# A fixed step for every piece of the blocks' preparation, its products in TensorE's written order, and GpSimd's row operations moved from blocks 2 and 3 to block 1

## The chip, the core and the metric

The kernel runs on one core of a Trainium2 chip. A core has TensorE (PE, matrix products), VectorE (DVE), ScalarE (ACT), GpSimd (POOL) and SyncE (SP, which issues most loads). Each engine takes its own instructions one after the other, in the order of its queue, and waits on semaphores for the others. The metric is the device time of one execution in microseconds. The kernel before took 1632.62 us (median of 3 runs, 1624.2 to 1632.76).

## The reference

Two neural blocks in sequence on 512 positions of 1024 channels, all in 32-bit floats. The change lies in the first one's recurrent mixer, which runs over 256 context positions and then over the 512 positions, forwards and backwards, for 8 heads of 64 channels:

```
def step(S, inp):
    r_t, w_t, kk_t, b_t, v_t, k_t = inp
    sa = jnp.einsum("bhvk,bhk->bhv", S, kk_t)
    S = (S * w_t[:, :, None, :] - sa[..., None] * b_t[:, :, None, :]
         + v_t[..., None] * k_t[:, :, None, :])
    return S, jnp.einsum("bhvk,bhk->bhv", S, r_t)
...
cb, cc, cx, r, k, v, w_lo, a_lo, g_lo = split_proj(h @ lp["w_in"])
y, finals = rwkv_scans(r, k, v, w_lo, a_lo, lp, init)
y_conv = cb * shortconv1d(cc * cx, lp["conv_a_w"])
y_rwkv = rwkv_output(y, r, k, v, g_lo, lp)
return jnp.concatenate([y_conv, y_rwkv], axis=-1) @ lp["w_out"], finals
```

After it come an output projection, a convolutional feed-forward network, the second block (a gated linear recurrence, windowed attention and another feed-forward network) and a norm.

## The kernel before

`proj` (L301) projects the inputs with `w_in` in column tiles of 128. Each 32-bit operand is split into a high part (ScalarE, L183) and a rest (L184, usually VectorE), and a tile is 24 products (`mm3`). In the tiles below 12 and in tile 25 the rest of a tile's second half is made by GpSimd. The last part of `proj` is the short convolution: for j = 0 to 3 the tiles 4+j, 8+j and j. Beside the tiles runs `ada12`, 32 row loads of 512 KB each with one VectorE operation of 128x1024.

The recurrence is cut into chunks of 64 positions, 12 in each direction, and the heads into 4 blocks of 2 heads. `rwkv` (L489) runs one `stage` (L767) of 12 steps for each block j. A step takes one chunk of each direction: products on TensorE, four to six copies on ScalarE (`R` L804, `U` L810, the state `S` L821, the output `Y`), which each wait for the product before and are waited for by the next. `look` (L723) works ahead: for each pair of chunks it makes products into PSUM (`psc`), which VectorE masks into `AS` (L747, COPY_PREDICATED), and transposed keys (`pkt`), which ScalarE copies; `psc` and `pkt` share three banks, tag "sc". A stage's products and `look`'s bear the token "pe" and keep their written order on TensorE.

Before its stage each block needs `prep` (L560), a generator that stops 29 times, so that it runs in 30 pieces: pieces 1 to 16 load keys, decays and low-rank weights, make products `pb`, `pl` and `pa` (L582, L592, L644) in one PSUM bank, and fill `KB` and `KR`; pieces 17 to 30 are `inverse` (L666), which inverts the 24 triangular 64x64 matrices of `AK`. Its core are 62 row operations (L688, L689), each needing the one before, on VectorE for blocks 0 and 1 and on GpSimd for blocks 2 and 3 (L682). Two transposes (`F`, L691 and L692) on VectorE follow, then copies into `XT` and products `pt` and `po` (L708, L715), whose result completes `XT`, the operand of the stage's third group of products.

`prep(0)` runs as one run inside `proj`. Blocks 1 to 3 stand in one chain: `RC` = 5 pieces after each j of the convolution, then `RB` = 4, 2 pieces in each step of stages 0 and 1. What is left after stage 1 is written at once; from stage 2 on the chain holds `splits` (five splits for the output projection) and `first` (its first weight tile). In the written order a step has a priority, `base + 200*g`, and a piece one that is put 105 to 118 later (`PF`). The scheduler that orders each engine's instructions goes by these priorities and by its own idea of when an operand is ready; only instructions of one token keep their order among themselves. `gn` (L841) is the group norm of a finished block, spread over the next stage's steps; two of its operations, `ys` and the power `grs`, are GpSimd's.

Of the kernel before, what the change touches and what calls it, by code (L numbers as in the profile page):

```python
# [18 lines left out]
P = 128  # L19
# [103 lines left out]
class K:  # L123
# [177 lines left out]
    def proj(self):  # L301
        nc, A, r1, p0 = self.nc, self.A, self.r1, self.p0
# [6 lines left out]
        for k in range(KD):  # L309
            e = nc.scalar if k % 2 else nc.sync  # L310
# [26 lines left out]
        bcc, _ = self.rsqrt_bc(acc[:, 0:NC_], NC_, 1.0 / 1024, 1e-6, self.pp)  # L337
# [6 lines left out]
        hc = [t[:, i, :] for tag, n in (("KB10", 6), ("KB11", 6), ("KR10", 5)) for t in [self.pp.tile([P, n, NC_], F32R, tag=tag, name="hc", bufs=1)] for i in range(n)]  # L344
        hhi = [[None] * KD, hc[:KD]]
        hlo = [[None] * KD, hc[KD:2 * KD]]
        piece = lambda u, k0: self.wsplit(A["win"][u][:, k0:k0 + 4], 4, P, eng=nc.gpsimd if k0 and not 12 <= u < 25 else None)
        ahead = {(24, k0): piece(24, k0) for k0 in (0, 4)}
        G = self.pp.tile([P, KD, 2], F32, tag="bo", name="G", bufs=2)
        for kc in range(KD):  # L350
# [4 lines left out]
            for i in range(2):  # L355
                g, sh = G[:, kc, i:i + 1], self.mod[:, kc, i:i + 1]
# [11 lines left out]
        def rows(n):  # L368
            for _ in range(n):
                next(ada, None)  # L370

        def tile_of(u, x=True, c=True):
            rows(1 if 12 <= u < 25 else 2)
            ws = [ahead.pop((u, k0), None) or piece(u, k0) for k0 in (0, 4)]
            w = lambda k: ws[k // 4](k % 4)
            out = []
            for on, i, n in ((x, 0, NX), (c, 1, NC_)):
                if on:
                    pm = self.psmm(n)
# [76 lines left out]
                r, hs = slice(64 * (i % 2), 64 * (i % 2) + 64), slice(64 * (i // 2), 64 * (i // 2) + 64)  # L456
                nc.sync.dma_start(out=self.vD[hs, :, 2 * tb + i % 2, :], in_=t.rearrange("p (j c) -> p j c", c=P)[r, :, hs])
        self.sets1()
        self.todo = self.prep(1)
        px, = tile_of(25, c=False)  # L460
        nc.scalar.activation(out=self.sg, in_=px, func=AF.Tanh, scale=0.5)
        nc.vector.tensor_scalar(out=self.sg, in0=self.sg, scalar1=0.5, scalar2=0.5, op0=ALU.mult, op1=ALU.add)
        for j in range(4):
            t = self.zx[j]
            pcc, = tile_of(4 + j, c=False)
            nc.scalar.activation(out=t, in_=pcc, func=AF.Copy)
            pcx, = tile_of(8 + j, c=False)
            u = r1.tile([P, NX + 2], F32, tag="u", name="u", bufs=1)
# [6 lines left out]
            pcb, = tile_of(j, c=False)  # L475
            nc.vector.tensor_tensor(out=t, in0=t, in1=pcb, op=ALU.mult)
            for _ in range(self.RC):
                next(self.todo, None)
        for _ in ada:
            pass  # L480

# [7 lines left out]
    def rwkv(self, es, ep):  # L489
        nc, r2 = self.nc, self.r2  # L490
        st = lambda name, shape: r2.tile([P] + shape, F32, name=name)
        self.AS = [[st(f"AS{d}{i}", [2, 192]) for i in range(3)] for d in range(2)]
        self.RU = [[st(f"RU{d}{i}", [2, 64]) for i in range(2)] for d in range(2)]
        self.S0 = [[st(f"S0{d}{i}", [64]) for i in range(2)] for d in range(2)]
        self.C1, self.C2 = [[self.ps2.tile([P, 512], F32, name=f"c{i}{d}") for d in range(2)] for i in (1, 2)]
        for t in (*self.AS[0], *self.AS[1]):
            nc.vector.memset(t, 0.0)
        todo, gn = self.todo, iter(())
        self.cells, self.vt, self.ahd = {}, {}, self.look()
        self.load_v(0)  # L500
        for _ in range(8):
            next(self.ahd)
        self.outs = []
        for j in range(4):
            if j < 2:
                todo = chain(todo, self.prep(j + 2))
            gn = self.stage(j, todo, self.RB[j], gn)
# [12 lines left out]
        for _ in todo:  # L520
            pass

        for _ in range(3):
            next(gn)
        for pm, w in self.ahead:
            self.mm3(pm, [(*w(k), self.ahi[k], self.alo[k]) for k in range(7)], last=False)
        for _ in gn:
            pass

    def splits(self):  # L530
        for k in range(5):
            self.split(self.ahi[k], self.alo[k], self.zx[k])
            yield

# [25 lines left out]
    def prep(self, j):  # L560
# [26 lines left out]
        for d in range(2):  # L587
# [51 lines left out]
            for q in range(2):  # L639
                pa = psm(384, "pa")  # L640
                for c in range(6 * q, 6 * q + 6):
                    kp = krc[:, c, :] if c < 4 else krx[:, c - 4, 0, :]
                    lt, rt_ = (kp, kb[:, c, bs, :]) if d else (kb[:, c, bs, :], kp)
                    self.mmh(pa[:, (c - 6 * q) * 64:(c - 6 * q) * 64 + 64], lt, rt_)  # L644
                n = 12 * d + 6 * q
                self.copy(nc.scalar, self.AK[:, n:n + 6, :], pa.rearrange("p (c t) -> p c t", t=64))
                yield
        yield from self.inverse(j)

# [16 lines left out]
    def inverse(self, j):  # L666
# [5 lines left out]
        XT, AK = self.S[j]["XT"], self.AK  # L672
# [19 lines left out]
        nc.vector.transpose(out=F2.rearrange("p n j -> p j n"), in_=X.rearrange("p i j -> p j i"))  # L692
        yield
        D = slice(0, 12), slice(12, 24)
        for r, F in zip(D, (F1, F2)):
# [7 lines left out]
        for r in D:  # L703
            yield
            pt = ps("pt")
            for n in range(r.start, r.stop):
                for h in range(2):
                    nc.tensor.matmul(pt[b1[h], n - r.start, :], AK[b0[h], n, 32:64], F2[b0[h], n, :], start=True, stop=True)  # L708
            for h in range(2):
                self.copy(nc.scalar, T[b1[h], r, :], pt[b1[h]])  # L710
        yield
        po = ps("po")
        for c in range(12):
            for h in range(2):
                nc.tensor.matmul(po[b0[h], c, :], T[b1[h], c, :], F1[b1[h], c, :], start=True, stop=True)  # L715
                nc.tensor.matmul(po[b1[h], c, :], F1[b1[h], 12 + c, :], T[b1[h], 12 + c, :], start=True, stop=True)
# [6 lines left out]
    def look(self):  # L723
# [3 lines left out]
        for j in range(4):  # L727
            for i in range(6):
# [9 lines left out]
                for d, (c0, kb, krs, A) in enumerate(part):  # L738
                    ps = self.ps2.tile([P, 2, N], F32, tag="sc", name="psc", bufs=3)
                    for c in range(2):  # L740
                        if c:
                            yield
                        self.mmh(ps[:, c, 0:W], kb[:, c0 + c, d], krs[c], order="pe")
                        if x:
                            self.mmh(ps[:, c, W:N], kb[:, c0 + c, 1 - d], krs[c][:, 64:P], order="pe")
                    m = self.c(f"m{d}").bitcast(I32)[:, 0:N]
                    nc.vector.copy_predicated(A[:, :, 0:N], m.unsqueeze(1).to_broadcast([P, 2, N]), ps)  # L747
# [16 lines left out]
        self.nc.sync.dma_start(out=vt, in_=self.vD[:, j])  # L764
        self.vt[j] = vt

    def stage(self, j, todo, rb, gn):  # L767

        nc, r2 = self.nc, self.r2
        XT, PC = self.S[j]["XT"], self.S[j]["PC"]  # L770
# [15 lines left out]
        for g in range(12):  # L786
# [45 lines left out]
                    self.load_v(j + 1)  # L832
            with self.prio(at + self.PG):
                next(gn, None)
            for i in range(rb):
                with self.prio(at + self.PF[j] + i * self.PK // rb):
                    next(todo, None)
        self.tc.cur_priority = base + 12 * self.PK
        return self.gn(j, Y, self.S[j]["bo"], self.vt[j])

    def gn(self, j, Y, bo, vt):  # L841
# [50 lines left out]
        if j < 3:  # L892
            pg = gate()
        nc.vector.tensor_tensor(out=z, in0=pg, in1=z, op=ALU.mult)
        if j:
            self.split(self.ahi[4 + j], self.alo[4 + j], z)


# [562 lines left out]
```

## Time and profile before

The profiled execution took 1635.69 us (its span from the first to the last instruction 1633.9 us), 3.07 us over the median of the runs.

| stretch of the span (us) | what runs | length |
|---|---|---|
| 0 to 281.9 | `proj` with `prep(0)` and most of `prep(1)` | 281.9 |
| 281.9 to 351.5 | stage 0 | 69.6 |
| 351.5 to 443.9 | stage 1 | 92.4 |
| 443.9 to 524.7 | stage 2 | 80.8 |
| 524.7 to 565 | stage 3 | 40.3 |
| 565 to 1633.9 | the rest of both blocks | 1068.9 |

A stage begins here with its first copy `R` (L804). The profile counts an engine as busy while an instruction runs, not while it waits. TensorE's granted clock is given as a share of 2.4 GHz and takes two levels, 1.2 and 2.4 GHz, so a mean of 0.75 over a stretch is half its time at either level.

### The profile page before, as it was taken

Reading aid. Unit: us, or ns where it says so; the run is one execution under the profiler, and the core shown is the slowest. Engines: PE = TensorE matmul, PEld = TensorE weight load, DVE = VectorE, ACT = ScalarE, POOL = GpSimd, SP = SyncE. Lnnn points to the kernel's source line nnn. Section 1 sums busy time; section 2 is a strip of 40 time slices with the busy share of each in tenths; the row PEclk is TensorE's granted clock in tenths of the full one; section 3 lists DMA queues with packets and bytes.
Section 4 is the critical chain, followed back from the end, with each engine's and each line's share of the span. In section 5 each row is a group of like instructions: output and inputs, shape, how many; then the busy total and the mean of one; then the engine's idle time right before and its main releaser. Section 6 shows DMA issues by size and latency. Waiting matters only on the chain. (4 is left out here: it accounts for less than half of the span.)

```text
span 1633.9 us, 29054 instructions
## 1 busy us (share of the span) xinstructions
PE 1493.1 (91%) x12062; PEld 1236.5 (76%) x12062; DVE 960.7 (59%) x1554; ACT 631.5 (39%) x1258; POOL 211.6 (13%) x278
## 2 busy tenths in 40 slices
PE   4999699874849999999999998899999999999998
PEld 2877577864748899888888886787777888888886
DVE  3768956652423267888884437678975555554221
ACT  3524243452516443333333324334554333332122
POOL 1121122046280000000000003121200000000000
PEclk9999899776868999999999999999999999999999
DMA  9577522010002042232332332221022322323221
GB/s 340 184 260 223 147 92 86 4 44 2 4 11 95 18 130 78 92 103 91 103 90 91 98 98 79 78 65 52 27 60 86 100 90 91 103 91 101 93 84 58
DMA packets 62181, 152.84 MB, mean 94 GB/s; under 512 B 12641, under 2 KB 14433, under 8 KB 62049
## 3 DMA queue, kind: packets, MB, share of 16 engines
q1 hardware_dynamic: 58016, 143.95, 27.7%
q10 hardware_dynamic: 4032, 7.04, 1.3%
q8 instruction: 94, 1.54, 0.4%
q14 instruction: 39, 0.31, 0.1%
HBM read 143.10 MB, written 7.86 MB: 92 GB/s over the span
## 5 line engine op out<-in xcount | busy, mean ns | idle before, releaser
L183 ACT ACTIVATE whi<-w 128x1024 fp32r<-128x1024 f32 (+2 forms) x220 | 208.8, 950 | 448.6 <-PE pm L170 323.3
L184 DVE TENSOR_TENSOR wlo<-w,whi 128x1024 fp32r<-128x1024 f32 (+2 forms) x199 | 220.5, 1109 | 168.5 <-ACT whi L183 166.7
L169 PE MATMUL pm<-ahi,whi 128*128 128x512 f32 (+1 forms) x624 | 237.0, 380 | 3.0 <-DVE sh L1144 2.6
L170 PE MATMUL pm<-alo,whi 128*128 128x512 f32 (+1 forms) x624 | 235.5, 377 | 0.0
L171 PE MATMUL pm<-ahi,wlo 128*128 128x512 f32 (+1 forms) x624 | 234.7, 376 | 0.0
L170 PE MATMUL pm<-al,whi 128*128 128x512 f32 x352 | 140.3, 399 | 0.0
L169 PE MATMUL pm<-ah,whi 128*128 128x512 f32 x352 | 139.9, 397 | 0.0
L171 PE MATMUL pm<-ah,wlo 128*128 128x512 f32 x352 | 139.8, 397 | 0.0
L169 PEld LDWEIGHTS pm<-ahi,whi 128*128 128x128 f32 x624 | 118.0, 189 | 24.4 <-ACT sh L1159 3.0
L171 PEld LDWEIGHTS pm<-ahi,wlo 128*128 128x128 f32 x624 | 118.0, 189 | 21.1 <-issue 0.7
L170 PEld LDWEIGHTS pm<-alo,whi 128*128 128x128 f32 x624 | 117.9, 189 | 20.1 <-issue 0.7
L1017 DVE SCALAR_TENSOR_TENSOR cv<-pm,vec,cv 128x441 f32<-128x441 f32 (+2 forms) x176 | 121.0, 693 | 4.1
L169 PEld LDWEIGHTS pm<-ah,whi 128*128 128x128 f32 x352 | 66.5, 189 | 15.8
L171 PEld LDWEIGHTS pm<-ah,wlo 128*128 128x128 f32 x352 | 66.5, 189 | 15.7 <-issue 0.2
L170 PEld LDWEIGHTS pm<-al,whi 128*128 128x128 f32 x352 | 66.5, 189 | 15.7 <-issue 0.2
L169 PE MATMUL pm<-hhi,whi 128*128 128x512 f32 x176 | 73.3, 417 | 4.7 <-ACT whi L183 4.6
L171 PE MATMUL pm<-hhi,wlo 128*128 128x512 f32 x176 | 71.5, 406 | 1.4 <-DVE wlo L184 1.4
L170 PE MATMUL pm<-hlo,whi 128*128 128x512 f32 x176 | 71.2, 405 | 0.0
L169 PE MATMUL pd<-whi,gh 128*128 128x512 f32 x176 | 69.6, 396 | 0.0
L170 PE MATMUL pd<-wlo,gh 128*128 128x512 f32 x176 | 69.5, 395 | 0.0
L171 PE MATMUL pd<-whi,gl 128*128 128x512 f32 x176 | 69.5, 395 | 0.0
L169 PE MATMUL pm<-hh,whi 128*128 128x512 f32 x176 | 69.3, 394 | 0.0
(399 smaller groups left out, 3060.7 us busy)
## 6 DMA issues: line engine op xcount, KB each, us to landing
w<-in_fup SPq DMA_DIRECT2D x44, 512.0 KB, 3.7
adaw<-in_adat SPq DMA_DIRECT2D x32, 512.0 KB, 4.6
w<-in_win SPq DMA_DIRECT2D x44, 256.0 KB, 3.6
w<-in_wg SPq DMA_DIRECT2D x22, 512.0 KB, 3.7
w<-in_wu SPq DMA_DIRECT2D x22, 512.0 KB, 3.7
w<-in_wd SPq DMA_DIRECT2D x22, 512.0 KB, 3.7
w<-in_win SPq DMA_DIRECT2D x18, 512.0 KB, 3.7
w<-in_wout SPq DMA_DIRECT2D x16, 512.0 KB, 3.7
```

The source lines that it names most:

```text
L169: nc.tensor.matmul(out, lh, rh, start=(first and i == 0), stop=False)
L170: nc.tensor.matmul(out, lh, rl, start=False, stop=False)
L171: nc.tensor.matmul(out, ll, rh, start=False, stop=(last and i == n - 1))
L183: self.nc.scalar.activation(out=hi, in_=src, func=AF.Copy)
L184: (eng or self.nc.vector).tensor_tensor(out=lo, in0=src, in1=hi.bitcast(F32), op=ALU.subtract)
L1017: nc.vector.scalar_tensor_tensor(out=o, in0=p[:, ro[0] + dr:ro[1] + dr, co[0] + dc:co[1] + dc], scalar=w(i), in1=o, op0=ALU.mult, op1=ALU.add)
```

## The change

Six edits. First, the chain and its counts go. A table `AT` names for each stage and step which block's preparation advances, and by how many pieces; in the convolution `prep(1)` advances by one piece before it and by two after each tile. So block 1 has 25 pieces written in `proj` and ends in step 9 of stage 0, block 2 ends in step 9 of stage 1 and block 3 in step 9 of stage 2. All pieces of a step have the priority `at + 110`. Second, `inverse` gives its row operations to GpSimd for block 1 and to VectorE for blocks 0, 2 and 3. Third, the products `pt` and `po` (and `pa` for blocks 2 and 3) take the token "pe"; the transposes `F` and `look`'s masked copies take a token "dv". The products `pb` and `pl` take none. Fourth, block 2 gets its own `AK2`, so that block 3's `pa` doesn't wait for block 2's inverse. Fifth, in `proj` VectorE makes every rest, and `ada12`'s rows are spread otherwise over the tiles (none at tiles 12 to 15, two at tile 24, 32 as before). Sixth, the preparation's memory is closed after stage 2 and not after stage 1, so `splits`, now six, and `first` move from stage 2 to the first seven steps of stage 3.

```diff
-    RB, RC = (4, 2, 1, 1), 5
+    AT = {(0, 0): (2, 2), (0, 1): (2, 2), (0, 2): (2, 2), (0, 4): (2, 4), (0, 5): (2, 2, 1, 1), ...
+    AT.update({(1, 10): (3, 1), (1, 11): (3, 2)})
...
+    AT.update({(3, g): (4, 1) for g in range(8)})
...
-        piece = lambda u, k0: self.wsplit(A["win"][u][:, k0:k0 + 4], 4, P, eng=nc.gpsimd if k0 and not 12 <= u < 25 else None)
+        piece = lambda u, k0: self.wsplit(A["win"][u][:, k0:k0 + 4], 4, P)
...
-            rows(1 if 12 <= u < 25 else 2)
+            rows(2 if u > 19 or u < 12 else u // 16)
...
-        self.todo = self.prep(1)
+        self.preps = [self.prep(i) for i in range(4)]
+        next(self.preps[1])
...
+            for _ in range(2):
+                next(self.preps[1])
...
-            if j == 1:
-                for _ in todo:
-                    pass
+            if j == 2:
                 ep.close()
...
-                todo = chain(self.splits(), self.first())
+                self.preps.append(chain(self.splits(), self.first()))
...
-        e = nc.vector if j < 2 else nc.gpsimd
+        e = nc.gpsimd if j == 1 else nc.vector
...
-        nc.vector.transpose(out=F1.rearrange("p n i -> p i n"), in_=X)
+        stamp(nc.vector.transpose(out=F1.rearrange("p n i -> p i n"), in_=X), "dv")
...
-            for i in range(rb):
-                with self.prio(at + self.PF[j] + i * self.PK // rb):
-                    next(todo, None)
+            with self.prio(at + 110):
+                do = self.AT.get((j, g), ())
+                for i, n in zip(do[::2], do[1::2]):
+                    for _ in range(n):
+                        next(self.preps[i], None)
```

GpSimd's queue before, where block 2's inverse begins in stage 1 (`vt`, `ys` are `gn`'s, `rk` is block 3's piece 1, `tmp` and `X` are the row operations):

```order
L849 TENSOR_TENSOR vt_2495<-vt_2495,bo_1128 128x512
L680 MEMSET X_3240 128x1024
L579 TENSOR_TENSOR rk_3801<-rt_3791,kt_3789 128x512
L681 MEMSET X_3240 128x32
L868 TENSOR_TENSOR ys_3885<-Y_2531,Y_2532 128x512
L688 TENSOR_TENSOR tmp_3239<-U_3238,X_3240 128x31
L689 TENSOR_TENSOR X_3240<-X_3240,tmp_3239 128x31
```

And now, where block 1's begins, in the convolution (`u` is the convolution's buffer for j = 3, `rk` block 2's piece 1):

```order
L609 MEMSET sg_2642 128x12
L587 TENSOR_TENSOR rk_2621<-rt_2611,kt_2609 128x512
L685 COPY AK_101<-AK_101 32x24x32 x2
L479 MEMSET u_2427 128x1
L480 MEMSET u_2427 128x1
L689 MEMSET X_2295 128x1024
L690 MEMSET X_2295 128x32
L697 TENSOR_TENSOR tmp_2294<-U_2293,X_2295 128x31
L698 TENSOR_TENSOR X_2295<-X_2295,tmp_2294 128x31
```

GpSimd's long run of row operations stands in the convolution, and in stages 1 and 2 its queue holds `gn`'s and `prep`'s single operations alone.

VectorE's queue before, around block 2's transposes in stage 1 (`gv`, `yc` belong to `gn`, `AS` are `look`'s masked copies):

```order
L880 TENSOR_SCALAR gv_4020<-gv_4020 128x8
L885 TENSOR_TENSOR yc_3955<-yc_3955,grs_4113 128x512
L747 COPY_PREDICATED AS02_2473<-cst_60,psc_3912 128x384
L747 COPY_PREDICATED AS12_2476<-cst_60,psc_3922 128x384
L747 COPY_PREDICATED AS00_2471<-cst_60,psc_4061 128x384
L747 COPY_PREDICATED AS10_2474<-cst_60,psc_4071 128x384
L691 STREAM_TRANSPOSE F1_3438<-X_3240 128x32x32
L692 STREAM_TRANSPOSE F2_3439<-X_3240 128x32x32
L194 COPY XT2_2470<-F1_3438 128x768
L194 COPY XT2_2470<-F2_3439 128x768
L747 COPY_PREDICATED AS01_2472<-cst_60,psc_4220 128x384
```

And now (`sg`, `cs` belong to block 3's preparation):

```order
L698 TENSOR_TENSOR X_3550<-X_3550,tmp_3549 128x4x28
L617 SCALAR_TENSOR_TENSOR cs_4088<-cst_60,sg_4003 128x780
L697 TENSOR_TENSOR tmp_3549<-U_3548,X_3550 128x87
L698 TENSOR_TENSOR X_3550<-X_3550,tmp_3549 128x3x29
L697 TENSOR_TENSOR tmp_3549<-U_3548,X_3550 128x60
L698 TENSOR_TENSOR X_3550<-X_3550,tmp_3549 128x2x30
L697 TENSOR_TENSOR tmp_3549<-U_3548,X_3550 128x31
L698 TENSOR_TENSOR X_3550<-X_3550,tmp_3549 128x31
L700 STREAM_TRANSPOSE F1_3971<-X_3550 128x32x32
L701 STREAM_TRANSPOSE F2_3972<-X_3550 128x32x32
L199 COPY XT2_2510<-F1_3971 128x768
L756 COPY_PREDICATED AS01_2512<-cst_60,psc_4115 128x384
```

The row operations stand in VectorE's queue between `look`'s masked copies, and the whole inverse stands ahead of `AS01`, the copy for chunks 8 and 9.

TensorE's queue before, where block 2's first `pt` stands: among `look`'s `psc` for chunks 8 and 9, in step 6 of stage 1 (`c20` with `RU` is that step's third group).

```order
L654 MATMUL c11_2486<-S010_2483,KR11_1681 64x64 x2
L654 MATMUL psc_4220<-KR10_1680,KB10_1678 64x128 x2
L654 MATMUL psc_4220<-KR10_1680,KB10_1678 64x64 x2
L708 MATMUL pt_3515<-F2_3439,AK_101 32x32 x24
L654 MATMUL psc_4230<-KR11_1681,KB11_1679 64x128 x2
L654 MATMUL psc_4230<-KR11_1681,KB11_1679 64x64 x2
L654 MATMUL c20_2487<-RU00_2477,zx_65 64x64 x2
```

And now, at the end of step 7 (`c10` with `AS01` begins step 8, `py` and `pg` are `gn`'s):

```order
L662 MATMUL c21_2530<-RU11_2520,AS10_2514 64x64 x2
L662 MATMUL py_4167<-cst_60,yc_3817 64x64 x3
L717 MATMUL pt_4263<-F2_3972,AK2_2525 32x32 x18
L662 MATMUL c10_2527<-vt_3260,AS01_2512 64x64 x2
L662 MATMUL c10_2527<-S000_2521,KR10_1670 64x64 x2
L662 MATMUL c11_2528<-vt_3260,AS11_2515 64x64 x2
L871 MATMUL pg_4260<-sg_69,gup_3617 128x512
```

Block 2's `pt` moved one step later, behind work that needs VectorE's next masked copy.

## Rows read from the trace of the kernel before

**Rows 1.** The page's 40 slices of the span, busy tenths, for GpSimd and TensorE's clock:

```profile
POOL 1121122046280000000000003121200000000000
PEclk9999899776868999999999999999999999999999
```

**Rows 2.** Busy time by stage (0 to 3): stretch, length, engines with instructions, clock, DMA:

```profile
281.90:351.50 69.60, 61.53 (x1422) 55.98 (x1422) 44.56 (x93) 36.67 (x126) 3.84 (x10) 0.77 0.05 14
351.50:443.90 92.40, 63.92 (x1492) 57.61 (x1490) 34.12 (x45) 37.70 (x129) 46.65 (x81) 0.74 0.04 13
443.90:524.70 80.80, 51.54 (x1346) 48.76 (x1342) 23.48 (x34) 33.68 (x120) 38.84 (x69) 0.75 0.17 53
524.70:565.00 40.30, 39.38 (x1101) 35.94 (x1095) 10.39 (x20) 22.57 (x100) 4.18 (x4) 1.00 0.02 6
```

**Rows 3.** Waits from 281 to 565 us: in total, times, longest:

```profile
PE pt L708 <- DVE F L692: 39.6, 3, 18.2
DVE F L691 <- POOL X L689: 34.5, 2, 18.8
DVE yc L885 <- POOL grs L883: 17.1, 3, 8.0
PE pkt L654 <- DVE AS L747: 10.2, 3, 6.0
```

**Rows 4.** Timeline in stage 1: start, length, what, idle time before and its releaser:

```profile
370.36 0.69 PE L654 MATMUL pkt<-cst,KB 64*64 64x64 f32 x8 [6.01 <-DVE AS L747]
...
396.78 1.90 DVE L691 STREAM_TRANSPOSE F<-X 128x1024 f32<-128x1024 f32 x1 [18.82 <-POOL X L689]
...
400.50 1.49 PE L708 MATMUL pt<-F,AK 32*32 32x32 f32 x48 [18.18 <-DVE F L692]
```

**Rows 5.** Row operations of blocks 1 and 2 (L688, then L689): busy time by engine:

```profile
281.00:309.00 28.00, 10.50 (x31) 0.00 (x0) 0.89 0.01 4
355.00:398.00 43.00, 0.00 (x0) 16.14 (x31) 0.70 0.04 10
...
281.00:309.00 28.00, 10.55 (x31) 0.00 (x0) 0.89 0.01 4
355.00:398.00 43.00, 0.00 (x0) 17.52 (x31) 0.70 0.04 10
```

**Rows 6.** Stretches of one clock level, columns as in Rows 2:

```profile
311.00:335.00 24.00, 23.09 (x430) 20.04 (x430) 6.76 (x9) 11.02 (x30) 1.94 (x5) 0.50 0.01 3
...
506.00:560.00 54.00, 52.89 (x1551) 49.36 (x1546) 17.05 (x29) 32.39 (x138) 3.92 (x3) 1.00 0.14 42
```

**Rows 7.** The copies R (L804, two a step): ACT busy (count), clock, DMA:

```profile
281.50:305.50 24.00, 3.14 (x14) 0.88 0.02 4
```

**Rows 8.** The 128x512 product of `pl` in stages 0 and 1:

```profile
L592 PE MATMUL pl<-lin,lh 128*128 128x512 f32 x8 | 4.9, 609 | 0.0
```

**Rows 9.** Transposes of the inverse in the stages (mean ns of one behind the bar):

```profile
L691 DVE STREAM_TRANSPOSE F<-X 128x1024 f32<-128x1024 f32 x3 | 5.7, 1905 | 34.5 <-POOL X L689 34.5
L679 DVE STREAM_TRANSPOSE U<-AK 128x1024 f32<-128x1024 f32 x2 | 3.9, 1972 | 0.9 <-ACT Y L190 0.9
```

**Rows 10.** Splits in stage 2 (L183 on ACT, then L184 on DVE and POOL):

```profile
498.00:512.00 14.00, 6.97 (x9) 0.85 0.45 144
...
498.00:512.00 14.00, 7.97 (x9) 0.00 (x0) 0.85 0.45 144
```

**Rows 11.** VectorE and GpSimd on the same tiles of the convolution, alone and together:

```profile
235.89 1.29 POOL L184 TENSOR_TENSOR wlo<-w,whi 128x512 fp32r<-128x512 f32 x1
...
230.00 2.04 POOL L184 TENSOR_TENSOR wlo<-w,whi 128x512 fp32r<-128x512 f32 x1 [3.28 <-ACT whi L183]
...
230.81 1.78 DVE L636 TENSOR_TENSOR KR<-rt,cs 128x512 f32<-128x512 f32 x1
...
L636 DVE TENSOR_TENSOR KR<-rt,cs 128x512 f32<-128x512 f32 x4 | 2.7, 678 | 0.0
```

**Rows 12.** The convolution for j = 2, when its second tile is done:

```profile
251.58 0.69 DVE L471 TENSOR_TENSOR u<-zx,pm 128x512 f32<-128x512 f32 x1 [0.51 <-PE pm L171]
```

More of the change, by code (lines that the diff above doesn't have):

```diff
@@ L465, in proj @@
             pcc, = tile_of(4 + j, c=False)
+            for _ in range(2):
+                next(self.preps[1])
             nc.scalar.activation(out=t, in_=pcc, func=AF.Copy)
             pcx, = tile_of(8 + j, c=False)
+            for _ in range(2):
+                next(self.preps[1])
             u = r1.tile([P, NX + 2], F32, tag="u", name="u", bufs=1)
@@ L475, in proj @@
             pcb, = tile_of(j, c=False)
+            for _ in range(2):
+                next(self.preps[1])
             nc.vector.tensor_tensor(out=t, in0=t, in1=pcb, op=ALU.mult)
-            for _ in range(self.RC):
-                next(self.todo, None)
         for _ in ada:
@@ L494, in rwkv @@
         self.S0 = [[st(f"S0{d}{i}", [64]) for i in range(2)] for d in range(2)]
+        self.AK2 = st("AK2", [32, 64])
+        nc.gpsimd.memset(self.AK2, 0.0)
         self.C1, self.C2 = [[self.ps2.tile([P, 512], F32, name=f"c{i}{d}") for d in range(2)] for i in (1, 2)]
@@ L497, in rwkv @@
             nc.vector.memset(t, 0.0)
-        todo, gn = self.todo, iter(())
+        gn = iter(())
         self.cells, self.vt, self.ahd = {}, {}, self.look()
@@ L504, in rwkv @@
         for j in range(4):
-            if j < 2:
-                todo = chain(todo, self.prep(j + 2))
-            gn = self.stage(j, todo, self.RB[j], gn)
-            if j == 1:
-                for _ in todo:
-                    pass
+            gn = self.stage(j, gn)
+            if j == 2:
                 ep.close()
@@ L516, in rwkv @@
                 self.alo = [pa.tile([P, NX], F32R, name=f"alo{i}") for i in range(8)]
-                todo = chain(self.splits(), self.first())
+                self.preps.append(chain(self.splits(), self.first()))
                 self.e3 = es.enter_context(ExitStack())
                 self.psa, self.axbufs = [self.psum(self.e3, "psa", side="right")], 1
-        for _ in todo:
+        for _ in self.preps[4]:
             pass
@@ L530, in splits @@
     def splits(self):
-        for k in range(5):
+        for k in range(6):
             self.split(self.ahi[k], self.alo[k], self.zx[k])
@@ L643, in prep @@
                     lt, rt_ = (kp, kb[:, c, bs, :]) if d else (kb[:, c, bs, :], kp)
-                    self.mmh(pa[:, (c - 6 * q) * 64:(c - 6 * q) * 64 + 64], lt, rt_)
+                    self.mmh(pa[:, (c - 6 * q) * 64:(c - 6 * q) * 64 + 64], lt, rt_, order="pe" if j > 1 else None)
                 n = 12 * d + 6 * q
-                self.copy(nc.scalar, self.AK[:, n:n + 6, :], pa.rearrange("p (c t) -> p c t", t=64))
+                self.copy(nc.scalar, (self.AK2 if j == 2 else self.AK)[:, n:n + 6, :], pa.rearrange("p (c t) -> p c t", t=64))
                 yield
@@ L671, in inverse @@
         big = lambda name: pp.tile([P, 32, 32], F32, tag="inv", name=name, bufs=3)
-        XT, AK = self.S[j]["XT"], self.AK
+        XT, AK = self.S[j]["XT"], self.AK2 if j == 2 else self.AK
+        stamp = lambda m, t: self.tc.stamp_issue_order_token(m.ins, t) if j else None
         b0, b1 = [slice(o, o + 32) for o in (0, 64)], [slice(o + 32, o + 64) for o in (0, 64)]
@@ L690, in inverse @@
         F1, F2 = big("F1"), big("F2")
-        nc.vector.transpose(out=F1.rearrange("p n i -> p i n"), in_=X)
-        nc.vector.transpose(out=F2.rearrange("p n j -> p j n"), in_=X.rearrange("p i j -> p j i"))
+        stamp(nc.vector.transpose(out=F1.rearrange("p n i -> p i n"), in_=X), "dv")
+        stamp(nc.vector.transpose(out=F2.rearrange("p n j -> p j n"), in_=X.rearrange("p i j -> p j i")), "dv")
         yield
@@ L707, in inverse @@
                 for h in range(2):
-                    nc.tensor.matmul(pt[b1[h], n - r.start, :], AK[b0[h], n, 32:64], F2[b0[h], n, :], start=True, stop=True)
+                    stamp(nc.tensor.matmul(pt[b1[h], n - r.start, :], AK[b0[h], n, 32:64], F2[b0[h], n, :], start=True, stop=True), "pe")
             for h in range(2):
@@ L714, in inverse @@
             for h in range(2):
-                nc.tensor.matmul(po[b0[h], c, :], T[b1[h], c, :], F1[b1[h], c, :], start=True, stop=True)
-                nc.tensor.matmul(po[b1[h], c, :], F1[b1[h], 12 + c, :], T[b1[h], 12 + c, :], start=True, stop=True)
+                stamp(nc.tensor.matmul(po[b0[h], c, :], T[b1[h], c, :], F1[b1[h], c, :], start=True, stop=True), "pe")
+                stamp(nc.tensor.matmul(po[b1[h], c, :], F1[b1[h], 12 + c, :], T[b1[h], 12 + c, :], start=True, stop=True), "pe")
         for h in range(2):
@@ L746, in look @@
                     m = self.c(f"m{d}").bitcast(I32)[:, 0:N]
-                    nc.vector.copy_predicated(A[:, :, 0:N], m.unsqueeze(1).to_broadcast([P, 2, N]), ps)
+                    self.tc.stamp_issue_order_token(nc.vector.copy_predicated(A[:, :, 0:N], m.unsqueeze(1).to_broadcast([P, 2, N]), ps).ins, "dv")
                     yield
@@ L765, in load_v, with stage @@
         self.vt[j] = vt
-    def stage(self, j, todo, rb, gn):
+    def stage(self, j, gn):
         nc, r2 = self.nc, self.r2
@@ L894, in gn @@
         nc.vector.tensor_tensor(out=z, in0=pg, in1=z, op=ALU.mult)
-        if j:
+        if j > 1:
             self.split(self.ahi[4 + j], self.alo[4 + j], z)
```

3 lines of the change are left out of this document (added).

## The prediction

> **What bounds the kernel now.** I read the slices first: GpSimd is nearly idle outside slices 9 to 11, and TensorE's clock is below its upper level from slice 7 to 12 and almost nowhere later [rows 1]. So the first third is the place. The table by stage comes next: stage 3, which has no preparation beside it, takes 40.3 us at clock 1.00; stages 0, 1 and 2 take 69.6, 92.4 and 80.8 us at 0.77, 0.74 and 0.75, with about as much work of their own [rows 2]. The list of waits says why: 39.6 us of TensorE's idle time ends with `F`, in three waits, and VectorE in turn waited 34.5 us for GpSimd's `X` in two of them [rows 3]. The timeline shows one such pair: `F` at 396.78 after 18.82 us, `pt` at 400.50 after 18.18 us [rows 4]. TensorE takes its queue in order, so the whole recurrence stands behind that `pt`, although nothing in the step needs it. A smaller wait has the same root: `gn`'s power sits in GpSimd's queue behind row operations, VectorE waits for it (17.1 us), masked copies stand behind that, and TensorE's `pkt` waits 10.2 us for them [rows 3]; one of these is the 6.01 us at 370.36 [rows 4]. Everything after 565 us is left alone.
>
> Around these waits the clock falls. At the lower level (1.2 GHz) 430 products took 24.0 us, 55.8 ns each; at the upper one 1551 took 54.0 us, 34.8 ns each [rows 6].
>
> **Row operations.** For one block VectorE is busy 10.50 + 10.55 = 21.1 us, GpSimd 16.14 + 17.52 = 33.7 us [rows 5]. On VectorE they do not stop the recurrence by themselves: in 281.5 to 305.5, most of block 1's, 14 copies `R`, 7 steps, went by in 24.0 us, 3.4 us a step [rows 7], the pace of stage 3 (40.3 / 12). So the swap removes GpSimd's run from stages 1 and 2, adds 21.1 us to VectorE in each and takes 21.1 us from it in stage 0.
>
> **Block 1 on GpSimd.** In the new order its pieces 14 to 19 stand in the convolution's j = 2, whose second tile was done at 251.6 [rows 12]. With `pa`, its copy, two copies of `AK` and the transpose (1.97 us [rows 9]) behind that, I put the first row operation at 257. 33.7 us of work and 6 us for pauses and collisions (an estimate, a sixth of the work) end it at 297; `F` takes 3.8 us [rows 9], so 301. TensorE's `pt` stands at step 7 of stage 0, at 281.9 + 7 x 4.5 = 313 by the stage time below. Cost: none, with 12 us in hand. Without that cover each late microsecond counts whole.
>
> **Stage 0.** The same 1422 products [rows 2] at 34.8 ns are 49.5 us. The 16 wide products `pl` (up to 609 ns where half the time was at the lower level [rows 8]) are longer than that mean: about 4 us more, bounds 0 and 8. VectorE falls to 44.6 - 21.1 = 23.5 us. The waits for the first masked copies stay, an estimated 1.5 us. Total 55, against 69.6.
>
> **Stage 1.** TensorE: 1492 x 34.8 ns + 4 = 55.9 us. VectorE: 34.1 us [rows 2], which holds two transposes `U` where one will stand there (-2.0), plus 21.1: 53.2 us. Two queues of 53 and 56 us that wait for each other through `psc` and `AS` don't overlap wholly: the order shows block 2's inverse and half of block 3's preparation ahead of `AS01` (step 8), and until that copy a bank stays full and `pkt` of step 7 can't begin. Bounds: 56 (all hidden) and 75 (20 us stay in series, half of what TensorE waits for `F` in the three stages today). I take 63, nearer to the hidden end because of the 24.0 us of [rows 7]; against 92.4.
>
> **Stage 2.** TensorE: 1346 x 34.8 = 46.8 us. VectorE: 23.5 - 8.0 (the splits, which leave [rows 10]) + 21.1 = 36.6 us. No front of another block, so a few microseconds of waits before `AS01` at most: 50, bounds 46.8 and 60; against 80.8.
>
> **Stage 3.** It takes ScalarE's 7.0 us and VectorE's 8.0 us of splits [rows 10]. VectorE has room (10.4 of 40.3 us busy). ScalarE is busy 22.6 [rows 2] and its copies carry the chain, so a split of 0.6 to 1 us ahead of an `R`, `U` or `S` delays it. Bounds 0 and 7; I take 2.7: 43 us. The loads move too: before, the first `wout` tiles landed before stage 3; now they wait for the preparation's memory to close, with 40 us left to land and be split, hidden by stage 3.
>
> **The rest.** VectorE gets the 13 halves that GpSimd split, at most 0.7 us each, in a convolution where TensorE is busy throughout: nothing, bounds -2 and 3. `ada12`'s rows keep their count and nearly their places: nothing. The new tokens cost no instruction; what they add is `F` and the masked copies in written order, counted above. `AK2` adds one memset on GpSimd behind block 1's row operations, with nothing of stage 0 before step 6 behind it.
>
> **The sum.** 55 + 63 + 50 + 43 = 211 us against 283.1: 72 us less. That is all at the upper clock level. Short waits will remain and some of them will be followed by a low stretch; one like 311 to 335 costs 24.0 x (1 - 34.8 / 55.8) = 9 us. I take one, bounds 0 and 27. So 63 us less than the profiled execution's 1635.69: 1572.7. That execution lay 3.07 us over the median of the runs, so 1570.
>
> **A rule against the change.** VectorE and GpSimd do slow each other: GpSimd's split, 1.29 us by itself, took 2.04 us where VectorE's `KR` product ran, and that one took 1.78 us where its mean is 0.68 [rows 11]. The Trainium skill (SBUF — State Buffer, Who interferes with whom) says that a VectorE instruction with two SBUF inputs and a GpSimd instruction that reads SBUF exclude each other, the later one standing still for the whole of the earlier. These rows agree.
>
> **Rivals.**
> - *Late GpSimd* (0.12). As in [rows 11], each operation of one engine holds up one of the other. In the new order some 25 operations of VectorE fall into GpSimd's run, of 0.68 us like `KR`'s or more, say 0.75. If each holds it for its length, that is 19 us and not a part of the 6: the run ends at 312, `F` at 316, and `AS01` for chunks 8 and 9 behind it, which step 7's `pkt` needs from 309 on. 10 us of wait and one more low stretch: 19 us worse, 1589. For it: the rows. Against it: GpSimd's own operations are 0.5 us on average, so VectorE often falls between them.
> - *All hidden* (0.13). Each stage runs at TensorE's own length and the clock stays up: 53.5 + 56 + 47 + 40.3 = 197, 86 us less, 1546. For it: stage 3 does so today [rows 2]. Against it: stage 1 has two equally long queues.
> - *The waits only move* (0.07). `pl`, `pb` and the transposes `U` bear no token, so the change doesn't fix every piece; TensorE then waits at them. Only the difference between the two engines is gained: 33.7 - 21.1 = 12.6 us in each of two waits, 25 us, and a few of `gn`'s: 1605.
> - *Slower* (0.06): VectorE's queue in series with the recurrence. Masked copies stand between row operations; if each batch ran only after `psc` and each `pkt` only after the batch, stages 0 to 2 would take VectorE's 23.5 + 53.2 + 36.6 = 113 us on top of TensorE's 55.5 + 56 + 47 = 158: 271, 28 us over today's 242.8, and stage 3 another 3: 1664. It decides from the point where three quarters of VectorE's 113 us stand in TensorE's way. For it: the 10.2 us that `pkt` waited for `AS` [rows 3]. Against it: [rows 7].
>
> **How the numbers follow.** The forecast has 0.62, its own range is 1553 to 1588 (stage 1 between 56 and 75, low stretches between 0 and 27 us). To hold 8 in 10 it must reach to half of the hidden case and over the late one: 1545 to 1603. A measurement of this kernel tells 0.5%, 8 us, from no change. Faster: 0.62 + 0.13 + 0.12 + nearly all of 0.07 = 0.92; slower 0.05; the same 0.03, from the edges of the last two.
>
> **What would show it.** Right: no wait of TensorE for `F` over 2 us; row operations of block 1 on GpSimd ending before 303; stage lengths near 55, 63, 50 and 43; VectorE busy about 53 us in stage 1; the mean clock of stages 0 to 2 over 0.85; stretches after stage 3 as long as before. Wrong: `pkt` waiting for `AS` by more than 10 us in stage 1, which would be the series case; `pt` of block 1 waiting in stage 0 (GpSimd late); or waits at `pl`. A mean clock that stays near 0.75 without waits over 4 us would break the sum at its last term.

## The result, and the profile after

| | before | after |
|---|---|---|
| median of the runs, us | 1631.27 (4 runs, 1624.20 to 1632.76) | 1586.74 (4 runs, 1584.02 to 1595.64) |
| profiled execution: device time, span, mean clock | 1635.69, 1633.9, 0.945 | 1584.02, 1582.2, 0.973 |

The ratio is 0.9745, 95% interval 0.9695 to 0.9795: about 42 us faster. The same kernel timed again beside later experiments (the repeat) gave 1587.76 (6 runs), ratio 0.9736 (0.9706 to 0.9765). The forecast was 1570 (range 1545 to 1603), a gain of 63 us where the medians show 44.5 and the two profiled executions 51.7.

The table by stage of the kernel after, columns as in [rows 2] (stretch, length, busy us with instruction counts of PE, PEld, DVE, ACT, POOL, clock, DMA share, GB/s):

```profile
277.50:345.00 67.50, 52.65 (x1402) 47.94 (x1404) 35.72 (x55) 35.04 (x124) 29.49 (x47) 0.87 0.08 22
345.00:413.30 68.30, 57.88 (x1472) 50.85 (x1470) 49.02 (x103) 37.35 (x128) 9.38 (x15) 0.93 0.04 10
413.30:473.20 59.90, 48.24 (x1352) 44.48 (x1348) 35.02 (x76) 29.77 (x117) 6.91 (x8) 0.91 0.12 37
473.20:515.90 42.70, 42.30 (x1097) 37.44 (x1097) 14.74 (x23) 25.76 (x104) 4.79 (x4) 1.00 0.18 55
```

Stages 0 to 3 took 69.6, 92.4, 80.8 and 40.3 us [rows 2] and now take 67.5, 68.3, 59.9 and 42.7: 44.7 us less. The other 7 us of the 51.7 between the spans lie outside: 4.4 ahead of the scan (the recurrence of stages 0 to 3), 2.6 behind it. GpSimd has left stages 1 and 2 and is busy in stage 0; the clock's mean is 0.87 to 0.93 where it was 0.74 to 0.77. The page's slices say the same, against [rows 1]:

```profile
POOL 1121015620110000000000014121200000000000
PEclk9999899899989999999999998999999999999999
```

TensorE's waits from 270 to 515 us (engine, line, tile, releaser: total, times, longest), against [rows 3]:

```profile
PE pa L662 <- ACT AK L195: 9.1, 4, 7.4
PE pkt L662 <- DVE AS L756: 6.2, 4, 4.3
PE c L662 <- ACT S L830: 5.9, 9, 2.6
PE po L724 <- issue: 3.4, 1, 3.4
```

The 39.6 us at `pt` are gone. Two single waits stand out now. The first is new, in stage 0; four pieces of the timeline show its chain (GpSimd, ScalarE, TensorE, VectorE):

```profile
300.58 1.81 POOL L506 MEMSET AK<- 128x2048 f32 x1
...
302.42 0.49 ACT L195 ACTIVATE AK<-pa 128x384 f32<-128x384 f32 x1 [7.25 <-POOL AK L506]
...
302.96 1.55 PE L662 MATMUL pa<-KR,KB 64*64 64x64 f32 x24 [7.36 <-ACT AK L195]
...
300.67 1.93 DVE L700 STREAM_TRANSPOSE F<-X 128x1024 f32<-128x1024 f32 x1 [6.07 <-POOL X L698]
```

GpSimd's row operations of block 1 ended at 300.6. Behind them in its queue is `AK2`'s memset; ScalarE's first copy of block 2's `pa` into `AK2` waits for it, the second `pa` waits for that copy's bank, and the recurrence stands behind `pa` in TensorE's written order. VectorE meanwhile stands at block 1's `F` for the same row operations. The second is in stage 2, where the kernel before had one of 3.93 us at the same tile (VectorE, then TensorE):

```profile
437.98 1.90 DVE L700 STREAM_TRANSPOSE F<-X 128x1024 f32<-128x1024 f32 x1
439.75 1.91 DVE L701 STREAM_TRANSPOSE F<-X 128x1024 f32<-128x1024 f32 x1
441.55 1.00 DVE L756 COPY_PREDICATED AS<-cst,psc 128x384 f32<-128x384 int32 x2
...
442.14 1.54 PE L662 MATMUL pkt<-cst,KB 64*64 64x64 f32 x24 [4.30 <-DVE AS L756]
```

VectorE runs block 3's row operations up to 437.98, then both transposes, and only then the masked copies that free `pkt`'s bank; the masked copy before these had started at 432.45.

### The profile page after: what moved, and what is told of

It is laid out like the page before. It is cut to its first block, busy times and chain, and to the rows that moved or that the text cites. A ratio compares the mean times of both kernels' runs of the same rounds, so it can differ in the third digit from the quotient of the medians.

```text
span 1582.2 us, 29037 instructions
## 1 busy us (share of the span) xinstructions
PE 1473.5 (93%) x12062; PEld 1216.7 (77%) x12062; DVE 984.1 (62%) x1629; ACT 629.7 (40%) x1258; POOL 172.0 (11%) x204
## 5 line engine op out<-in xcount | busy, mean ns | idle before, releaser
L189 DVE TENSOR_TENSOR wlo<-w,whi 128x1024 fp32r<-128x1024 f32 (+2 forms) x212 | 230.2, 1089 | 181.2 <-ACT whi L188 179.4
L175 PE MATMUL pm<-al,whi 128*128 128x512 f32 x352 | 137.1, 389 | 0.0
L174 PE MATMUL pd<-whi,gh 128*128 128x512 f32 x176 | 69.6, 396 | 0.0
L174 PE MATMUL pm<-hh,whi 128*128 128x512 f32 x176 | 69.3, 394 | 0.0
```

What stands on the lines that cost most here:

```text
L174: nc.tensor.matmul(out, lh, rh, start=(first and i == 0), stop=False)
L175: nc.tensor.matmul(out, lh, rl, start=False, stop=False)
L189: (eng or self.nc.vector).tensor_tensor(out=lo, in0=src, in1=hi.bitcast(F32), op=ALU.subtract)
```

## The experiments

Theory: the gain is the swap's (GpSimd's slow row operations out of stages 1 and 2); what is short of the forecast is block 1 ending late on GpSimd, and VectorE's queue in stage 2. Rivals: the fixed steps or the written order carry the gain; or the shortfall is TensorE's own. All medians in us, ratios to the kernel before run on the same chip (medians 1628.0 to 1629.6); stage lengths are from the first copy `R` of a stage to that of the next.

| kernel | median | ratio, 95% | stages 0, 1, 2 |
|---|---|---|---|
| after, again | 1587.76 | 0.9736 (0.9706-0.9765) | 63.8, 68.1, 62.0 |
| e1 | 1585.11 | 0.9741 (0.9718-0.9763) | 61.7, 69.4, 63.5 |
| e2 | 1583.43 | 0.9724 (0.9698-0.9750) | 57.3, 69.3, 62.0 |
| e3 | 1604.58 | 0.9855 (0.9833-0.9877) | 55.7, 84.3, 75.2 |
| e4 | 1594.57 | 0.9801 (0.9781-0.9821) | 54.7, 61.8, 62.0 |
| e5 | 1594.67 | 0.9815 (0.9785-0.9845) | 56.0, 69.1, 63.5 |
| e6 | 1599.32 | 0.9842 (0.9813-0.9872) | 84.2, 69.0, 62.1 |
| e7 | 1575.66 | 0.9701 (0.9666-0.9736) | 53.1, 62.5, 63.6 |
| e8 | 1577.37 | 0.9692 (0.9666-0.9718) | 68.1, 65.1, 55.4 |
| e9 | 1589.95 | 0.9748 (0.9719-0.9777) | 68.8, 62.1, 68.3 |
| e10 | 1577.03 | 0.9672 (0.9641-0.9703) | 52.0, 62.0, 61.4 |
| e11 | 1569.67 | 0.9613 (0.9585-0.9641) | 56.1, 62.7, 56.4 |

### Which part carries the gain: e6, e9, e3

e6 is the kernel before with the swap alone, e9 the kernel before with every block's rows on VectorE:

```diff
-        e = nc.vector if j < 2 else nc.gpsimd
+        e = nc.gpsimd if j == 1 else nc.vector     # e6
+        e = nc.vector                              # e9
```

> The kernel before, with the engine of the row operations alone changed as in the kernel after (GpSimd for block 1, VectorE for 0, 2 and 3). Theory A: the waits at pt in stages 1 and 2 (39.6 us together) are GpSimd's pace, so the swap by itself takes most of them away, and gives some back in stage 0, where block 1's operations now stand on GpSimd: 1600 to 1615. Theory B: the waits come from the order in which the pieces are dealt out, and a faster engine for the rows only moves them: 1624 to 1640.

> The kernel before with the row operations of all blocks on VectorE, nothing else changed. Theory A: GpSimd's pace is what the waits at pt were; without it stages 1 and 2 fall to the 69 and 62 us that they had with the swap alone, and stage 0 keeps its 69.6: 1590 (1583 to 1597). What the fixed steps then add is the rest to the 1583 with steps, order and all rows on VectorE. Theory B: in the old dealing VectorE is late with 62 more operations in stages 1 and 2, PE waits there for its copy_predicated: 1600 to 1615.

e6 came out at 1599.3, 0.7 us below its range; stages 1 and 2 are already as short as in the kernel after. Stage 0 grew to 84.2: the old dealing starts block 1's rows at 275.8, 1 us ahead of the scan, and TensorE waits 21.9 us at `pt` for them. In stages 1 and 2 the waits at `pt` fall from 18.2 and 17.5 us to 5.3 and 2.2 (e6, same view as before):

```profile
PE pt L708 <- DVE F L692: 29.5, 3, 21.9
PE pkt L654 <- DVE AS L747: 6.5, 7, 1.5
```

The kernel after lies 12 us under e6, and their intervals do not meet. So with block 1 on GpSimd the swap gives some 29 of the 42 us, and the other parts of the change together give the rest, nearly all of it in stage 0.

e9 came out at 1589.95 on a forecast of 1590, its lengths dealt out otherwise than expected. The waits at `pt` fall to 8.5 us, 4.0 of them in stage 0 as in the kernel before (e9, same view):

```profile
PE pt L708 <- DVE F L692: 8.5, 3, 4.0
```

So GpSimd's rows were 31 of the 39.6 us. One word in the kernel before gives as much as the whole change: its interval (0.9719 to 0.9777) covers both ratios of the kernel after. That does not make the rest of the change worthless: e10 (below), which has the table of steps and most other edits on top of e9 but no written order, is 13 us faster than e9, with intervals that do not meet. In the kernel after, block 1 on GpSimd and the written order cost about what the steps gain.

e3 is the converse, the kernel after with the old engines:

```diff
-        e = nc.gpsimd if j == 1 else nc.vector
+        e = nc.vector if j < 2 else nc.gpsimd
```

> Row operations of blocks 0 and 1 on VectorE and of 2 and 3 on GpSimd, as in the kernel before, with the fixed steps and written order of the kernel after. Theory A: PE's waits at pt in stages 1 and 2 were GpSimd's slow row operations of blocks 2 and 3 (33.7 us a block in the trace before, 44.3 in the trace after), which fixed steps do not hide wholly: stages 1 and 2 are 10 to 25 us longer together than in the kernel after, 1595 to 1615. Theory B: the fixed steps alone took the waits away, whichever engine does the rows: 1580 to 1590.

With all the steps and the order, stages 1 and 2 are 31 us longer than in the kernel after (29 than in its repeat), more than the 10 to 25 expected, and the time is in theory A's range. No wait at `pt` is left in it; TensorE now waits where `gn` is late, because its operations queue on GpSimd between row operations (`pv`, 14.6 us), and its clock falls to 0.82 and 0.77 in stages 1 and 2:

```profile
PE pv L662 <- POOL vt L860: 14.6, 3, 7.3
PE pkt L662 <- DVE AS L756: 9.0, 4, 3.6
```

### Why stage 0 gave little: e1, e2, e5

e1 moves the memset alone, e2 takes all rows to VectorE:

```diff
-        nc.gpsimd.memset(self.AK2, 0.0)
+        nc.vector.memset(self.AK2, 0.0)            # e1
-        e = nc.gpsimd if j == 1 else nc.vector
+        e = nc.vector                              # e2
```

> The memset of AK2 moves from GpSimd's queue (behind block 1's row operations) to VectorE's (ahead of AS's memsets). Theory A: in stage 0 PE's 7.4 us wait at pa of block 2 was this memset, and the 13.7 us of half clock from 298.2 followed from that idle time; both go: stage 0 from 67.5 to 55-60 us, the time from 1586.7 to about 1577 (1572 to 1581). Theory B: stage 0 is late because block 1's row operations themselves end at 300.6 on GpSimd, and F, XT and pt behind them hold the step; then PE waits the same time at another tile, and the time stays within 3 us of 1587.

> All blocks' row operations on VectorE, the fixed steps and written order kept. Theory A (the steps and the written order carry the gain, the move of block 1 to GpSimd little): VectorE takes block 1's 62 operations in about 21 us where it has room around the start of the scan, AK2's memset is no longer late, and the time lies between 1575 and 1590. Theory B (block 1 on GpSimd is a main part of the gain): the scan starts later or stage 0 is longer by the 21 us that VectorE has more to do, and the time is 1600 to 1608.

e1 missed: 1585.1, the case of theory B. The 7.4 us wait did go and another took its place (VectorE, ScalarE, TensorE in e1's timeline):

```profile
304.22 1.98 DVE L700 STREAM_TRANSPOSE F<-X 128x1024 f32<-128x1024 f32 x1 [5.83 <-POOL X L698]
...
311.60 0.84 ACT L620 ACTIVATE sg<-cs 128x768 f32<-128x768 f32 x1 [6.08 <-DVE cs L617]
...
312.86 0.80 PE L600 MATMUL pl<-lin,lh 128*128 128x512 f32 x1 [5.77 <-ACT ta L602]
```

`F` waits for the rows, block 2's scan `cs` is behind `F` on VectorE, ScalarE's exponential waits for `cs`, and `pl` for ScalarE. The two waits run side by side from one cause, so e1, which removes one, leaves the other. e2 removes the cause: stage 0 falls to 57.3, from 67.5 and 63.8 in the two traces of the kernel after. In time e2 is only some 4 us under the kernel after, within the intervals: from the convolution's first `u` to the start of stage 3 e2 takes 259.5 us, the kernel after 263.6 and 261.8. Some 3 us go back in the convolution, where VectorE now has block 1's rows as well, and 1 us in stage 1. So the 7.4 us at `pa` are not what the late block costs; with the rows where they are fast the kernel is at most some 4 us faster, and that is not clear of noise.

e5 undoes another part, proj's halves:

```diff
+        piece = lambda u, k0: self.wsplit(..., 4, P, eng=nc.gpsimd if k0 and not 12 <= u < 25 else None)
```

> The kernel after, with proj's second half pieces split on GpSimd again, as before. Theory A: this part is worth nothing (the prediction's term: 0, -2 to 3), and the 4.4 us by which the scan starts earlier in the trace after are a difference between two executions of the same work ahead of it: 1584 to 1590. Theory B: the 4.4 us are this part's, GpSimd's row operations of block 1 stand behind those splits as well and F is later still: 1591 to 1600.

Theory B, 8 us slower, but not by its reason: the halves queue behind the row operations on GpSimd, and proj's own products wait for them (12.4 us). The scan starts at 299.3 (277.5 and 281.1 in the kernel after's two traces):

```profile
PE pm L176 <- POOL wlo L189: 12.4, 2, 6.9
```

e10 asks the same without rows on GpSimd, on top of e7 (below):

> All rows on VectorE, no written order, and proj's second halves split on GpSimd as in the kernel before. With block 1's rows on GpSimd those halves cost 8 us (PE waited 5.5 us for a wlo that stood behind the row operations). Theory A: they cost only because GpSimd had the rows as well: within 4 us of the same kernel with the halves on VectorE (1575.7), or a little faster since VectorE has less to do ahead of the scan. Theory B: the halves on GpSimd are slow by themselves: 1581 to 1587.

1577.0 against e7's 1575.7: theory A. The halves' place matters only where GpSimd also has block 1. The repeat of the kernel after settles the rest of e5's question:

> The kernel after once more, beside the others of this call. Theory A: its time is 1583 to 1592, and the second trace shows the first copy R of the scan some 11 us behind the last u of the convolution, as in the first (10.7), with the absolute start anywhere from 277 to 283: the 4.4 us earlier start is execution to execution. Theory B: the scan starts at 277 to 278 again, the earlier start belongs to the change.

Its scan started at 281.1, 10.6 us behind the last `u`, as in the first trace. So most of the 4.4 us ahead of the scan are execution to execution, as theory A had it. So is the length of stage 0: the wait at `pa` is 7.4 us in both traces, but the stage took 67.5 us at clock 0.87 in the first and 63.8 at 0.95 in the second:

```profile
PE pa L662 <- ACT AK L195: 9.2, 4, 7.4
```

### The written order: e4, e7

e4 leaves out the order tokens that the change adds; e7 does so with all rows on VectorE:

```diff
-        stamp = lambda m, t: self.tc.stamp_issue_order_token(m.ins, t) if j else None
+        stamp = lambda m, t: None
-                    self.mmh(..., order="pe" if j > 1 else None)
+                    self.mmh(..., order=None)
-                    self.tc.stamp_issue_order_token(nc.vector.copy_predicated(...).ins, "dv")
+                    nc.vector.copy_predicated(...)
```

> The steps of the table and the row operations as in the kernel after, but pa, pt, po, F and copy_predicated are no longer held to the written order on TensorE and VectorE. Theory A: the order keeps copy_predicated ahead of the row operations and the blocks' products behind the scan's; without it PE waits more at the scan's own products: 5 to 20 us slower (1592 to 1607). Theory B: the table of steps alone decides, the scheduler finds the same order: within 4 us of 1587.

> All row operations on VectorE and the products, F and copy_predicated not held to the written order. Without the written order alone the scan started at 303.8, but its stages 0 and 1 took 54.7 and 61.8 us (67.5 and 68.4 with it). Theory A: the late start was F of block 1, which then stood ahead of the convolution's last products on VectorE and waited for GpSimd; with the rows on VectorE it goes, and the shorter stages stay: 1572 (1566 to 1579). Theory B: those stages were shorter only because the late start had given the preparation of blocks 1 and 2 more time ahead of them; then the time is that with the rows on VectorE in the written order, 1580 to 1588.

e4 is 8 us slower, as theory A's sign has it, by another road: `F` of block 1 moved on VectorE ahead of the convolution's last product and stood there for GpSimd, the first masked copy stood behind it, and TensorE waited 26.0 us at the scan's start. VectorE in e4's timeline:

```profile
295.95 1.93 DVE L700 STREAM_TRANSPOSE F<-X 128x1024 f32<-128x1024 f32 x1 [25.52 <-POOL X L698]
```

and TensorE in its list of waits from 267 to 310 us:

```profile
PE c L662 <- DVE AS L756: 26.0, 1, 26.0
```

With the rows on VectorE that wait goes and stages 0 and 1 stay short (53.1 and 62.5): e7, theory A. So among these kernels the written order helps only against GpSimd's late block. Without GpSimd e7 lies 8 us under e2 (intervals 0.9666-0.9736 and 0.9698-0.9750 overlap), with stage 1 at 62.5 against 69.3. That difference in stage 1 stands in every trace of these steps with rows of blocks 2 and 3 whole on VectorE: 68.1 to 69.4 with the order (after, its repeat, e1, e2, e5), 61.8 to 62.7 without it (e4, e7, e10, e11).

### VectorE's queue in stage 2: e8, e11

```diff
-        for k in range(31):
+        for k in range(0, 31, 2 if j > 1 else 1):     # e8, on the kernel after
-            if k % 4 == 0:
+            if k % 4 == 0 or j == 3 and k == 30:      # e11, on e7
```

> The kernel after, with every second row of the inverse left out for blocks 2 and 3 (30 of the 62 operations of each), some 10 us less on VectorE in stage 1 and in stage 2 each. Theory A: what made stages 1 and 2 longer than forecast is VectorE's queue (pkt waits 4.3 us at 437.8 for a copy_predicated that stands behind F's transposes), and the low clock that follows such waits: stage 2 falls from 59.8 to 50-54, stage 1 from 68.4 to 63-66, the time to 1575 (1571 to 1580). Theory B: they are as long because of TensorE's own products and short waits in the chain of RU and S, which VectorE doesn't set: within 4 us of 1587.

> All rows on VectorE and no written order, and block 3's last row and F one piece later in the table, so that on VectorE one of the two copy_predicated stands between F's two transposes and not behind both. Theory A: PE's wait at pkt in stage 2 (4.2 us) falls by about the 1.9 us of one transpose, block 3 has room before stage 3: 1573 (1569 to 1577). Theory B: what is gained there comes back at the end of stage 2, where pt and po of block 3 stand later and stage 3 waits for XT: 1576 to 1582.

e8 cut VectorE to 41.6 us in stage 1 and 25.3 in stage 2; the wait of 4.3 us is gone, the stages are 3.3 and 4.4 us shorter, 1577.4: theory A, though stage 2's 55.4 is over its 50 to 54 (TensorE's waits in e8 from 400 to 530 us):

```profile
PE pkt L662 <- DVE AS L756: 1.1, 2, 0.6
```

e11 goes at the same queue with all the work done, on e7. One masked copy now stands between the two transposes (e11, VectorE, then TensorE):

```profile
428.56 1.90 DVE L700 STREAM_TRANSPOSE F<-X 128x1024 f32<-128x1024 f32 x1
430.33 0.56 DVE L756 COPY_PREDICATED AS<-cst,psc 128x384 f32<-128x384 int32 x1
430.80 2.00 DVE L701 STREAM_TRANSPOSE F<-X 128x1024 f32<-128x1024 f32 x1
...
430.94 0.68 PE L662 MATMUL pkt<-cst,KB 64*64 64x64 f32 x16 [2.49 <-DVE AS L756]
```

The wait of 4.2 us in e7 became 2.49 and, for the second half, 1.67: it was split, not shortened. Still stage 2 fell from 63.6 to 56.4 (e7, then e11, columns as in [rows 2]):

```profile
398.70:462.40 63.70, 52.04 (x1352) 47.66 (x1348) 35.30 (x77) 30.29 (x117) 7.00 (x8) 0.84 0.11 35
403.60:459.90 56.30, 46.54 (x1350) 43.51 (x1345) 34.35 (x75) 28.96 (x115) 6.26 (x8) 0.91 0.13 40
```

TensorE's idle time fell by 1.9 us and the time of the same products by 5.5, at a clock of 0.91 for 0.84. The `pt` and `po` of block 3 stand a step later as well, and the 3.3 us that TensorE waited at `po` became 1.28 at another product. So the time is in theory A's range and its mechanism, a shorter wait at `pkt`, is not what the trace shows; which of the two, the split wait or the later `po`, kept the clock up was not tried. At 1569.67 e11 is the fastest kernel of the study, its interval below that of the kernel after.

## Why the prediction was right, and where it was too large

- **Where the time was.** Right: `pt`'s 39.6 us are gone, and e6 and e9 show that GpSimd's row operations were the cause of 31 of them. The 4.0 us in stage 0 and some 2 us in each of stages 1 and 2 stay in e9 and go only with the other parts of the change.
- **"`AK2` adds one memset on GpSimd behind block 1's row operations, with nothing of stage 0 before step 6 behind it."** This step failed. Block 2's `pa` stands in step 4 and is copied into `AK2`; ScalarE was ready for that copy at 295, and the memset ended at 302.4: a wait of 7.36 us for TensorE that the sum held at nothing. But e1 shows that this memset is not what the time hangs on: without it the time is the same.
- **"Cost: none, with 12 us in hand."** Failed with it. The run began at 256.3 (257 forecast) and took 44.3 us where 39.7 stood: 39.6 busy and 4.8 of pauses. `pt` did have time in hand; what had none was VectorE, which stops at `F` with block 2's scan behind it. Only `pt` was checked for who waits for `F`, not VectorE's own queue (e1). Stage 0 took 67.5 against 55. That its products' 52.65 meet the 53.5 is luck: the stage ran at 0.87, and in the repeat, at 0.95, they took 48.96. VectorE was busy 35.7 us where 23.5 stood, for the table puts 20 of block 2's row operations and a transpose `U` into stage 0, and beside GpSimd `KR`'s product of 128x512 took 0.92 us where it took 0.68 before. The rival "late GpSimd" had the late run and nearly the time (1589), with the run's end and `F` 12 us too late and the wrong place; that its time is so near is luck too, since e2 gives back only some 4 us.
- **Stage 1.** 68.3 against 63, within its bounds (56 to 75). TensorE 57.88 (55.9), VectorE 49.02 (53.2). No long wait; 10.4 us of short ones. The excess goes with the written order: without it the stage takes 62 us (e4, e7, e10, e11). The prediction had the order's cost "counted above"; how the order makes the stage longer stays open.
- **Stage 2.** 59.9 against 50, at the edge of its bounds (46.8 to 60), and 62.0 in the repeat, outside them. Work right (48.24 for 46.8, 35.02 for 36.6); "a few microseconds of waits before `AS01` at most" was too small: 4.3 at `pkt`, 3.4 at `po`, and low clock after them.
- **The clock.** Means 0.87, 0.93 and 0.91 over stages of 67.5, 68.3 and 59.9 us are 38 us at the lower level; at the prediction's rate that costs 14 us, where one stretch of 24 us (9) was taken. In the repeat (0.95, 0.95, 0.86) it is 31 us, dealt out otherwise.
- **Stage 3, the rest.** 42.7 against 43. Outside the stages the change is worth nothing, as forecast; the 7 us there belong to those executions, for the median gain is 44.5 us and the profiled one 51.7. In the repeat the scan starts 0.8 us earlier than in the kernel before, not 4.4; and from stage 3's first `R` to the end e6 and e9, which have the old code there, take 1104.9 and 1106.5 us where the profiled kernel before took 1109.2.
- **A rule against the change.** The row read for it was not the whole of it: ahead of `KR` VectorE's product `KB` (229.94 to 230.89) stood in the way of GpSimd's split of 230.00, and the split then in the way of `KR`. The conclusion holds.
- **The sum.** The stages took 238.4 us for 220 forecast (211 and 9). Read off this trace, 7.4 of these 18 are `pa`'s wait and 5 the clock (14 for 9); the other 6 are of the order of the waits at `pkt` and `po` in stage 2 (7.7). The runs split it otherwise: from the kernel after (1587) block 1 to VectorE gives 4 us (e2), leaving out the written order 8 more (e7), block 3's `F` a piece later 6 more (e11, 1570). Each of the first two steps is within the noise, all three together are far outside it. That e11 meets the forecast of 1570 is a coincidence: it is another kernel.

## What to carry to other kernels

When work moves to a slower engine, list everything queued behind it there and on every engine that will wait for its result, up to the next instruction that the critical engine needs; a margin at one consumer says nothing of the others. Two waits with one cause don't add, and removing one uncovers the other, so test the cause. And before building a schedule around a slow engine, try the one-word version that leaves the work where it is fast: here it gave the same time as the whole change, and with it the written order was no longer needed. The schedule paid on top of that (e10 is 13 us faster than e9), which a test of the whole change alone could not show.

## What the runs showed of the hardware

GpSimd's operations are held up by VectorE's scan. In the kernel after, one row operation took 2.08 us where the ones of its size around it took 0.64 to 0.68, while the scan of 128x780 ran on VectorE from 277.22 (GpSimd, then VectorE):

```profile
276.08 0.68 POOL L698 TENSOR_TENSOR X<-X,tmp 128x255 f32<-128x255 f32 x1
...
277.76 2.08 POOL L698 TENSOR_TENSOR X<-X,tmp 128x256 f32<-128x256 f32 x1
...
277.22 2.10 DVE L615 TENSOR_TENSOR_SCAN cs<-cst,sg 128x780 f32<-128x780 f32 x1
```

The rule of the Trainium skill (SBUF — State Buffer, Who interferes with whom), that a two-input VectorE instruction shuts out a GpSimd one that reads SBUF, agrees with this pair. In the repeat, e1, e3, e5 and e8 one row operation under such a scan took 1.74 to 2.16 us. The forecast's "a sixth" for pauses and collisions (6 us) became a third of the 33.7 us (10.7): 4.8 of pauses and 5.9 by which the operations themselves were longer.

TensorE's 3.4 us at `po` in stage 2 end with no releaser in the trace. They stand in the middle of a row of ready products, while 512 KB tiles of `wout` land; in e8 they stand there too. The records of the transfers narrow it down: during the gap (459.86 to 463.25) a 16 KB load of the instruction queue (q8) runs from 460.91 to 461.94. All eleven traces with such a gap, e11's of 1.28 us at another product among them, have such a load, and the gap ends 1.2 to 1.5 us behind it. So TensorE probably waited for its own instructions, whose load ran beside the weight loads; no run moved either load, so this is argued and not shown.
